# Output projections, dilated-attention values and v: 512-column products over two 512-row weight units in place of 256-column ones

## The chip, the cores and the metric

The kernel runs on one core of a Trainium2 chip. The metric is the device time of one execution in microseconds (us), the median of several runs. The engines are named as in the profile: PE (TensorE, matrix products), PEld (its weight loads), DVE (VectorE), ACT (ScalarE), POOL (GpSimd) and SP (SyncE, which issues the DMAs).

## The reference, cut to what matters

The input x is [1, 1024, 1024] in float32: 1024 tokens of 1024 channels. Three blocks follow each other.

1. `first_block`: a norm, a wide input projection, four mixers side by side (sparse attention, differential attention, retention, a state-space mixer), then `x + mixed @ w_out` and a norm.
2. The second block: an input projection, an RWKV-7 recurrence and a gated convolution side by side, `x + cat @ w_out_2`, and `x + relu(h @ w_ff1)**2 @ w_ff2`, then a norm.
3. The third block works on X = norm(x). A spatial gating branch takes `v = gelu(X @ w_v)` (2048 channels), normalises it, mixes it over tokens and multiplies it with two other projections. A dilated-attention branch has q, k and `vb = X @ w_vb` (1024 channels) for 8 heads. Both go through a projection and a gate each and are summed to m; the output is `x + norm(m @ w_out_3)`.

All matrix products are computed to float32 precision.

## The kernel before

Tokens are cut into 8 tiles of 128 and two halves of 512. An activation that feeds a product stands transposed on chip, as `(hi, lo)`: `hi` is the value rounded to float32r and `lo` the exact rest, each [128, 8 k tiles, 512 tokens] (`act_half`). Weights come in units (`wunit`): one DMA of 1 MB into `wraw`, then ACT makes `whi` (L183) and DVE makes `wlo` (L184), in two halves of 1024 columns each. The unit's three buffers come from a ring of six buffers of 9 KB per partition, so two units fit. A product runs in three passes, hi·hi, hi·lo and lo·hi, for each of its 128-row k tiles (`mm3`, all its matmuls are on L251); with 8 k tiles that is 24 matmuls into one PSUM bank. The profile names a matmul `out<-moving,stationary`.

There are two ways round. `cm` keeps the weights stationary and streams 512 tokens; the result is transposed, and the row reads `mm<-ahi,whi 128x512`. `tm`, and the code in its manner, keeps 128 tokens stationary and streams 256 columns of the weights; the result has tokens on partitions, and the row reads `mm<-whi,ahi 128x256`. Five places use the second way with 256 columns:

- `out_proj` after the first block (called from `first_to_second`): for each of 4 weight units of 256 columns, 4 token tiles, DVE adds the residual (L1629); twice, for two token halves. It is woven step by step with the norms of the next block.
- `out_proj` after RWKV (from `second_to_third`), the same.
- `vb_proj`: pairs of units, for each half and unit 4 token tiles; the result is copied by ACT or DVE (L1722 and L1724) to a buffer `vo` and stored to DRAM (L1725). It is woven with the final norm of block 2, which makes its input X tile by tile.
- `v_proj`: 8 units, for each 8 token tiles; ACT applies GELU (L1924), DVE takes statistics (L1925), SP stores (L1926). It has two PSUM banks.
- the last product of `merge`: ACT squares and sums (L2049), DVE multiplies by the norm's weights (L2050), then come the norm's factor and the output.

PSUM has 8 banks; `set_banks` gives each tag its banks, and `psum(tag)` goes round them. The order of the instructions on each engine is not that of the code: the program is built with a scheduler that plays the program on its own timeline, takes from all code what is ready, and so moves work of one stage into gaps of another. Each engine then executes its list strictly in order, and so does SP's queue of DMA issues. In the RWKV stage, `keep` adds products for nothing that hold their place (L172).

## Time and profile before

| quantity | value |
|---|---|
| runs shown | 3983.67, 3992.8 and 3976.47 us, median 3983.67 |
| profiled execution, span from first to last instruction | 3985.3 us |
| profiled execution, own time outside that span | not listed; the span lies inside the range of the runs |
| PE busy | 3836.2 us, 96% |
| PE weight loads busy | 3287.1 us, 82% |
| DVE, ACT, POOL busy | 2131.0, 1243.3, 539.5 us |
| mean granted TensorE clock | 0.966 of full speed |
| DMA queue 1 | 300.39 MB, 24.3% of 16 engines |

Matmuls overlap in the record: one lasts from its issue to its modelled end, and the next starts before that. So the time that a matmul takes of PE is read from the distance between two starts, not from its duration. The granted clock has two levels, 1.2 GHz (0.5) and 2.4 GHz (1.0).

The five stages of the change lie, in us of the span, at about 748 to 880 (first output projection), 1421 to 1605 (second one, with the end of RWKV), 2292 to 2398 (values of the dilated attention), 2852 to 3064 (v) and 3844 to 3985 (last product). RWKV is at 1131 to 1504.

### The profile page before, as it was taken

What the parts mean: (1) busy time and instruction counts of PE and PEld (TensorE: products, weight loads), DVE (VectorE), ACT (ScalarE), POOL (GpSimd) and SP (SyncE); (2) the same over time, 40 slices, a digit from 0 to 9 for tenths busy, and PEclk for the clock granted to TensorE, in tenths of its full rate; (3) what the DMA queues carried; (4) which work ended last, traced back from release to release, by engine and by line L of the source; (5) the groups of instructions that cost most, each with busy time, mean ns of one, the idle gap of its engine ahead of it and who ended that gap; (6) DMA issues with size and microseconds to landing.
All of it is one profiled execution on the core that took longest, in us unless ns stands there. A gap on an engine that the chain in (4) does not pass through costs nothing.

```text
span 3985.3 us, 57578 instructions
## 1 busy us (share of the span) xinstructions
PE 3836.2 (96%) x22592; PEld 3287.1 (82%) x22592; DVE 2131.0 (53%) x4925; ACT 1243.3 (31%) x2589; POOL 539.5 (14%) x825
## 2 busy tenths in 40 slices
PE   7999999799979989999999999999999999999998
PEld 6788888797868879888888898878899888888897
DVE  5356479668987865544444654444423444433154
ACT  4444436442232434222212232333422111121232
POOL 1011124300043410000000011111201211210000
PEclk9999999799977889999999999999999999999999
DMA  5321342431221233111111132112133222211143
GB/s 147 121 65 51 84 140 73 135 112 55 94 58 38 47 92 120 48 53 43 53 43 53 59 120 59 45 48 59 50 109 92 62 63 60 74 48 48 54 154 121
DMA packets 341697, 304.07 MB, mean 76 GB/s; under 512 B 51182, under 2 KB 305970, under 8 KB 341426
## 3 DMA queue, kind: packets, MB, share of 16 engines
q1 hardware_dynamic: 341426, 300.39, 24.3%
q8 instruction: 178, 2.92, 0.3%
q14 instruction: 93, 0.76, 0.1%
HBM read 234.27 MB, written 61.34 MB: 74 GB/s over the span
## 4 chain that ended last, share of the span: by engine, by line
PE 62%; DVE 2%; DMA 2%; ACT 1%; issue 1%; SPq 0%; POOL 0%; DVEq 0%; ACTq 0%; POOLq 0%
PE mm L251 54%; PE s L1798 2%; PE s L1972 1%; PE o L1820 1%; PE o L1872 1%; PE t L1865 0%; DMA wraw<-in_w_in_dram 0%; PE t L1897 0%; PE t L1842 0%; PE t L213 0%; DVE wlo L184 0%; PE o L1520 0%; PE f L172 0%; DMA alo<-ybT 0%; PE t L1465 0%
## 5 line engine op out<-in xcount | busy, mean ns | idle before, releaser
L251 PE MATMUL mm<-ahi,whi 128*128 128x512 f32 x2464 | 967.1, 394 | 0.5 <-ACT ahi L216 0.5
L251 PE MATMUL mm<-alo,whi 128*128 128x512 f32 x2464 | 965.3, 392 | 0.0
L251 PE MATMUL mm<-ahi,wlo 128*128 128x512 f32 x2464 | 963.4, 391 | 0.3 <-DVE wlo L184 0.3
L251 PE MATMUL mm<-whi,ahi 128*128 128x256 f32 (+2 forms) x1856 | 538.6, 291 | 16.4 <-ACT ahi L1612 7.5
L251 PEld LDWEIGHTS mm<-ahi,whi 128*128 128x128 f32 x2464 | 465.3, 189 | 96.9 <-ACT ahi L216 0.9
L251 PEld LDWEIGHTS mm<-ahi,wlo 128*128 128x128 f32 x2464 | 464.1, 188 | 97.0 <-DVE wlo L184 1.1
L251 PEld LDWEIGHTS mm<-alo,whi 128*128 128x128 f32 x2464 | 464.6, 189 | 94.1 <-issue 0.4
L183 ACT ACTIVATE whi<-wraw 128x1024 fp32r<-128x1024 f32 (+2 forms) x300 | 302.8, 1055 | 765.5 <-DMA wraw<-in_w_ff_dram 318.0
L251 PE MATMUL mm<-wlo,ahi 128*128 128x256 f32 (+2 forms) x1856 | 537.2, 290 | 1.8 <-DVE wlo L184 1.7
L251 PE MATMUL mm<-whi,alo 128*128 128x256 f32 (+2 forms) x1856 | 533.6, 289 | 2.0 <-DVE alo L218 1.5
L184 DVE TENSOR_TENSOR wlo<-wraw,whi 128x1024 fp32r<-128x1024 f32 (+2 forms) x300 | 357.5, 1229 | 332.6 <-PE mm L251 322.4
L251 PEld LDWEIGHTS mm<-whi,ahi 128*128 128x128 f32 x1856 | 358.2, 193 | 24.7 <-ACT ahi L1612 7.9
L251 PEld LDWEIGHTS mm<-wlo,ahi 128*128 128x128 f32 x1856 | 359.2, 194 | 7.6 <-issue 3.8
L251 PEld LDWEIGHTS mm<-whi,alo 128*128 128x128 f32 x1856 | 357.1, 193 | 6.1 <-issue 2.5
L1678 DVE TENSOR_TENSOR xm<-xm,mm 128x512 f32<-128x512 f32 x256 | 173.9, 686 | 120.1 <-PE mm L251 119.9
L251 PE MATMUL mm<-whi,ah 128*128 128x512 f32 x512 | 202.3, 395 | 0.0
L251 PE MATMUL mm<-wlo,ah 128*128 128x512 f32 x512 | 202.1, 395 | 0.0
L251 PE MATMUL mm<-whi,al 128*128 128x512 f32 x512 | 202.1, 395 | 0.0
L1170 DVE SCALAR_TENSOR_TENSOR cva<-cvh,vecs,cva 128x1022 f32<-128x1022 f32 (+29 forms) x120 | 145.4, 1263 | 0.2
L1660 DVE TENSOR_TENSOR fr<-fr 128x512 f32<-128x512 f32 x64 | 44.2, 690 | 154.1 <-ACT fr L1659 154.1
L207 POOL TENSOR_SCALAR x<-x,rT 128x1024 f32<-128x1024 f32 x16 | 18.8, 1174 | 760.9 <-PE mm L251 673.2
L251 PEld LDWEIGHTS mm<-whi,al 128*128 128x128 f32 x512 | 96.5, 188 | 22.5
(577 smaller groups left out, 5786.2 us busy)
## 6 DMA issues: line engine op xcount, KB each, us to landing
wraw<-in_w_in_dram SPq DMA_DIRECT2D x41, 1024.0 KB
wraw<-in_w_ff_dram SPq DMA_DIRECT2D x32, 1024.0 KB
wraw<-in_w_in_dram SPq DMA_DIRECT2D x59, 512.0 KB
wraw<-in_w_out_dram SPq DMA_DIRECT2D x24, 1024.0 KB
gv<-go SPq DMA_DIRECT2D x64, 128.0 KB
vl<-gv SPq DMA_DIRECT2D x16, 512.0 KB
wraw<-in_w_proj_a_dram SPq DMA_DIRECT2D x8, 1024.0 KB
wraw<-in_w_proj_b_dram SPq DMA_DIRECT2D x8, 1024.0 KB
```

The costliest lines, as they stand in the source:

```text
L183: nc.scalar.activation(hi, src, AF.Copy)
L184: nc.vector.tensor_tensor(lo, src, hi.bitcast(F32), op=OP.subtract)
L207: nc.gpsimd.tensor_scalar(xn, xt, rs, 1.0, op0=OP.mult, op1=OP.mult)
L251: nc.tensor.matmul(out, lhs[a][:, kl, ls], rhs[b][:, kr, rs], start=first and n == 0, stop=last and n == tot - 1)
L1170: nc.vector.scalar_tensor_tensor(a[:, 30 - j:], h[:, 0:994 + j], wj, a[:, 30 - j:], op0=OP.mult, op1=OP.add)
L1660: nc.vector.tensor_tensor(r, r, r, op=OP.mult)
L1678: nc.vector.tensor_tensor(xm[t][:, ns], xm[t][:, ns], q, op=OP.add)
L1798: nc.tensor.matmul(q[:, :256], qk[:, a, qcol], qk[:, b, kcol], start=n == 0, stop=n == 2)
L1820: nc.tensor.matmul(ob[:, 128 * (b % 4):128 * (b % 4 + i1 - i0)], vt[:w, cc + 1], pt[:, 128 * i0:128 * i1], start=b % 4 == 0 and cc == b - ...
L1872: nc.tensor.matmul(o[:, 256 * (r % 2):256 * (r % 2) + 256], vg[:, r, kb], pt[:, 256 * kb:256 * kb + 256], start=kb == 0, stop=kb == 1)
L1972: nc.tensor.matmul(q[:, 128 * t:128 * t + 128], vl[:, 4 * hf + t], wt, start=True, stop=True)
```

## The change

In the five places a product streams 512 columns of weights in place of 256. A weight unit still holds 1 MB, but as 512 rows (4 k tiles) by 512 columns in place of 1024 rows by 256 columns. A PSUM tile is now a whole bank and its sum runs over two units: 12 matmuls with the first (`kh == 0`), 12 with the second. `out_proj` and `merge` go over 4 token tiles with one unit, then over the same 4 with the next, so four banks are open at a time. `vb_proj` does so for each half with both units on chip. `v_proj` keeps its two banks and goes over pairs of token tiles. What follows on ACT and DVE is done on 512 columns at a time, except in `vb_proj`, where ACT copies one half of a tile and DVE the other. `merge` gets six banks for its products in place of four. Comments and docstrings are dropped too, which leaves no trace in the program. The diff, cut to its core:

```diff
--- before
+++ after
@@ out_proj, rows of x + A @ w for one token half @@
-    for u in range(4):
-        W = c.wunit([w[:, 256 * u:256 * u + 256]])
-        us = slice(256 * u, 256 * u + 256)
-        for i in range(4):
-            q = c.psum("mm")
-            c.mm3(q[:, :256], A, W, slice(i * 128, i * 128 + 128), slice(0, 256), [(k, k) for k in range(8)])
-            nc.vector.tensor_tensor(xs[i][:, us], xs[i][:, us], q[:, :256], op=OP.add)
-            yield
+    for nh in range(2):
+        ns = slice(512 * nh, 512 * nh + 512)
+        q = []
+        for kh in range(2):
+            W = c.wunit([w[512 * kh:512 * kh + 512, ns]], ktiles=4)
+            for i in range(4):
+                if kh == 0:
+                    q.append(c.psum("mm"))
+                c.mm3(q[i], A, W, slice(i * 128, i * 128 + 128), slice(0, 512), [(4 * kh + k, k) for k in range(4)],
+                      first=kh == 0, last=kh == 1)
+                if kh:
+                    nc.vector.tensor_tensor(xs[i][:, ns], xs[i][:, ns], q[i], op=OP.add)
+                yield
@@ vb_proj @@
-        for g in range(2):
-            W = [c.wunit([self.cols("vb", 256, 256 * u)]) for u in (2 * g, 2 * g + 1)]
+        for nh in range(2):
+            W = [c.wunit([self.cols("vb", 512, 512 * nh)[512 * kh:512 * kh + 512]], ktiles=4) for kh in range(2)]
             for hf in range(2):
-                for i in range(2):
-                    u = 2 * g + i
-                    for t in range(4 * hf, 4 * hf + 4):
-                        q = c.tm(W[i], slice(0, 256), X, t)
-                        o = tmp.tile([128, 256], F32, tag="vo", name=c.nm("vo"), bufs=2)
-                        if t % 2:
-                            nc.vector.tensor_copy(o, q[:, :256])
-                        else:
-                            nc.scalar.activation(o, q[:, :256], AF.Copy)
-                        nc.sync.dma_start(self.vb[t * 128:t * 128 + 128, 256 * u:256 * u + 256], o)
+                q = []
+                for kh in range(2):
+                    for t in range(4):
+                        if kh == 0:
+                            q.append(c.psum("mm"))
+                        c.mm3(q[t], X[hf], W[kh], slice(t * 128, t * 128 + 128), slice(0, 512),
+                              [(4 * kh + k, k) for k in range(4)], first=kh == 0, last=kh == 1)
+                        for i in range(2 * kh):
+                            r = 512 * hf + 128 * t
+                            o = tmp.tile([128, 256], F32, tag="vo", name=c.nm("vo"), bufs=2)
+                            x = q[t][:, 256 * i:256 * i + 256]
+                            if i:
+                                nc.vector.tensor_copy(o, x)
+                            else:
+                                nc.scalar.activation(o, x, AF.Copy)
+                            nc.sync.dma_start(self.vb[r:r + 128, 512 * nh + 256 * i:512 * nh + 256 * i + 256], o)
                         yield
@@ v_proj @@
-        st = p.tile([128, 8, 8, 6], F32, name="vstat")
-        for u in range(8):
-            W = c.wunit([self.cols("v", 256, 256 * u)])
-            for t in range(8):
-                q = c.tm(W, slice(0, 256), X, t)
-                o = p.tile([128, 256], F32, tag="vo", name=c.nm("go"), bufs=3)
-                nc.scalar.activation(o, q[:, :256], AF.Gelu_apprx_tanh)
-                nc.vector.bn_stats(st[:, t, u], o)
-                nc.sync.dma_start(self.gv[t * 128:t * 128 + 128, 256 * u:256 * u + 256], o)
+        st = p.tile([128, 8, 4, 6], F32, name="vstat")
+        for u in range(4):
+            W = [c.wunit([self.cols("v", 512, 512 * u)[512 * kh:512 * kh + 512]], ktiles=4) for kh in range(2)]
+            for t0 in range(0, 8, 2):
+                q = [c.psum("mm") for _ in range(2)]
+                for kh in range(2):
+                    for i in range(2):
+                        t = t0 + i
+                        c.mm3(q[i], X[t // 4], W[kh], slice((t % 4) * 128, (t % 4) * 128 + 128), slice(0, 512),
+                              [(4 * kh + k, k) for k in range(4)], first=kh == 0, last=kh == 1)
+                for i in range(2):
+                    t = t0 + i
+                    o = p.tile([128, 512], F32, tag="vo", name=c.nm("go"), bufs=2)
+                    nc.scalar.activation(o, q[i], AF.Gelu_apprx_tanh)
+                    nc.vector.bn_stats(st[:, t, u], o)
+                    nc.sync.dma_start(self.gv[t * 128:t * 128 + 128, 512 * u:512 * u + 512], o)
@@ merge, its last product; third_block @@
-            for u in range(4):
-                us = slice(256 * u, 256 * u + 256)
-                W = c.wunit([ins["w_out_3"][0][:, us]])
-                for i in range(4):
-                    q = c.psum("mm")
-                    c.mm3(q[:, :256], mh, W, slice(i * 128, i * 128 + 128), slice(0, 256), [(k, k) for k in range(8)])
-                    sq = tmp.tile([128, 256], BF, tag="fsq", name=c.nm("sq"), bufs=1)
...
+            for nh in range(2):
+                ns = slice(512 * nh, 512 * nh + 512)
+                q = []
+                for kh in range(2):
+                    W = c.wunit([ins["w_out_3"][0][512 * kh:512 * kh + 512, ns]], ktiles=4)
+                    for i in range(4):
+                        if kh == 0:
+                            q.append(c.psum("mm"))
+                        c.mm3(q[i], mh, W, slice(i * 128, i * 128 + 128), slice(0, 512), [(4 * kh + k, k) for k in range(4)],
+                              first=kh == 0, last=kh == 1)
...
+        c.set_banks(mm=[0, 1, 2, 3, 6, 7], t=[4, 5])
         with pool("mrg") as tmp:
             b.merge(ps, out, tmp)
```

How the order moves, at three places. First PE at the start of the first output projection, where products of `out_proj` (mm, weights whi and wlo, activations ahi and alo) are put between the last steps of differential attention (o, t), and of the state-space mixer (do; its result is turned by L824). Before:

```order
L251 MATMUL mm_8430<-wlo_8343,ahi_8313 128x256
L251 MATMUL mm_8430<-whi_8342,alo_8314 128x256
L788 MATMUL o_7021<-vv_5997,dAT_7221 128x64
L770 MATMUL t_7252<-ident,ws_6027 128x128 x4
L1051 MATMUL do_8247<-ws_5998,xbcB_7753 128x64 x4
L1054 MATMUL do_8247<-sst_8230,xbcB_7753 128x128 x2
L770 MATMUL t_7259<-ident,ws_6027 128x128
L788 MATMUL o_7021<-vv_5997,dAT_7257 128x64 x4
L251 MATMUL mm_8464<-whi_8457,ahi_8313 128x256
L788 MATMUL o_7021<-vv_5997,dAT_7261 128x64
```

Now:

```order
L251 MATMUL mm_8391<-wlo_8343,ahi_8313 128x512
L251 MATMUL mm_8391<-whi_8342,alo_8314 128x512
L788 MATMUL o_7021<-vv_5997,dAT_7221 128x64
L770 MATMUL t_7252<-ident,ws_6027 128x128 x4
L1051 MATMUL do_8247<-ws_5998,xbcB_7753 128x64 x4
L1054 MATMUL do_8247<-sst_8230,xbcB_7753 128x128 x2
L770 MATMUL t_7259<-ident,ws_6027 128x128
L788 MATMUL o_7021<-vv_5997,dAT_7257 128x64 x4
L788 MATMUL o_7021<-vv_5997,dAT_7261 128x64
L251 MATMUL mm_8475<-whi_8468,ahi_8313 128x512
```

The 20 products that stand between the two L788 rows (the last two of them are shown) have kept their places at twice the width. Before the turn L824, six products of the next column unit have become one.

The second place is ACT in `v_proj`: GELU results `go`, and the splits of weight units. Before:

```order
L1924 ACTIVATE go_26557<-mm_26532 128x256
L1868 ACTIVATE mpg_26316<-t_26311 128x512
L1924 ACTIVATE go_26586<-mm_26561 128x256
L1924 ACTIVATE go_26623<-mm_26598 128x256
L183 ACTIVATE whi_27071<-wraw_27070 128x1024 x2
L1924 ACTIVATE go_26652<-mm_26627 128x256
L1924 ACTIVATE go_26681<-mm_26656 128x256
L1924 ACTIVATE go_26710<-mm_26685 128x256
L1924 ACTIVATE go_26739<-mm_26714 128x256
```

Now:

```order
L1942 ACTIVATE go_25300<-mm_25250 128x512
L1879 ACTIVATE mpg_25084<-t_25079 128x512
L1942 ACTIVATE go_25304<-mm_25251 128x512
L1942 ACTIVATE go_25358<-mm_25308 128x512
L183 ACTIVATE whi_25375<-wraw_25374 128x1024 x2
L1942 ACTIVATE go_25362<-mm_25309 128x512
L1974 ACTIVATE wt_26163<-t_26161 128x128
L183 ACTIVATE whi_25615<-wraw_25614 128x1024 x2
L1942 ACTIVATE go_25432<-mm_25382 128x512
```

Before, one unit's split stands within a run of eight GELUs, a whole unit ahead of its use. Now a unit's split stands at the end of its pair's predecessor: whi_25375 is the second half of the rows for the next 512 columns, whose first product is go_25432's.

The third place is POOL in the RWKV stage, whose code is unchanged: lnx and lny belong to the convolution's norm, all others to RWKV. Before:

```order
L1233 TENSOR_SCALAR lnx_11646<-lnx_11646 128x512
L1234 TENSOR_TENSOR lny_11649<-lny_11649,lnx_11646 128x512
L1340 TENSOR_SCALAR ws_11287<-ws_11287 128x512
L1373 TENSOR_TENSOR ws_11287<-ws_11287 128x512
L1346 TENSOR_SCALAR ws_11289<-ws_11287,vecs_625,ka_11271 128x128 x4
L1233 TENSOR_SCALAR lnx_11683<-lnx_11683 128x512
L1234 TENSOR_TENSOR lny_11686<-lny_11686,lnx_11683 128x512
L1377 TENSOR_TENSOR ws_11285<-rk_11882,rk_11883 128x512
L1423 COPY ws_11288<-ws_11286 64x256
```

Now:

```order
L1361 TENSOR_TENSOR ws_10871<-ws_10871,s_2316_11549 128x512
L1234 TENSOR_TENSOR lny_11233<-lny_11233,lnx_11230 128x512
L1340 TENSOR_SCALAR ws_10871<-ws_10871 128x512
L1373 TENSOR_TENSOR ws_10871<-ws_10871 128x512
L1346 TENSOR_SCALAR ws_10873<-ws_10871,vecs_625,ka_10855 128x128 x4
L1377 TENSOR_TENSOR ws_10869<-rk_11466,rk_11467 128x512
L1233 TENSOR_SCALAR lnx_11267<-lnx_11267 128x512
L1423 COPY ws_10872<-ws_10870 64x256
L1385 TENSOR_TENSOR ws_10873<-ws_10873,ws_10871 128x512
```

The work is the same, but from here on the scheduler has put the RWKV steps of POOL, ACT, DVE, PE and SP in another sequence.

## Rows read from the trace of the kernel before

**Rows 1.** The page of the whole run: busy time by engine, and 40 slices.
```profile
PE 3836.2 (96%) x22592; PEld 3287.1 (82%) x22592; DVE 2131.0 (53%) x4925; ACT 1243.3 (31%) x2589; POOL 539.5 (14%) x825
...
PEclk9999999799977889999999999999999999999999
```

**Rows 2.** Groups by line and form, engine PE: count, busy us, mean ns.
```profile
L251 PE MATMUL mm<-whi,ahi 128*128 128x256 f32 x1536 | 440.2, 288 | 12.0 <-ACT ahi L1612 7.5 <-ACT whi L183 2.1 <-DVE y L1577 0.8
L251 PE MATMUL mm<-wlo,ahi 128*128 128x256 f32 x1536 | 438.4, 286 | 1.8 <-DVE wlo L184 1.7
L251 PE MATMUL mm<-whi,alo 128*128 128x256 f32 x1536 | 435.8, 286 | 2.0 <-DVE alo L218 1.5 <-DVE alo L1613 0.5
```

**Rows 3.** Timeline of PE in the v stage (start us, duration us, instruction).
```profile
2899.80 0.28 PE L251 MATMUL mm<-wlo,ahi 128*128 128x256 f32 x1
...
2906.52 0.28 PE L251 MATMUL mm<-whi,ahi 128*128 128x256 f32 x1
```

**Rows 4.** Timeline of PE in the last stage, 512 columns.
```profile
3799.74 0.39 PE L251 MATMUL mm<-ahi,wlo 128*128 128x512 f32 x1
...
3805.86 0.39 PE L251 MATMUL mm<-alo,whi 128*128 128x512 f32 x1
```

**Rows 5.** Timeline of PE in the feed-forward's second product.
```profile
1999.61 0.40 PE L251 MATMUL mm<-whi,al 128*128 128x512 f32 x1
...
2002.41 0.40 PE L251 MATMUL mm<-whi,al 128*128 128x512 f32 x1
```

**Rows 6.** Timeline of PE at the first output projection's start.
```profile
755.06 0.41 PE L251 MATMUL mm<-whi,ahi 128*128 128x256 f32 x1
...
758.69 0.41 PE L251 MATMUL mm<-whi,alo 128*128 128x256 f32 x1
```

**Rows 7.** Waits there: engine and line that waited <- releaser: us, times, longest.
```profile
PE mm L251 <- ACT ahi L1612: 6.8, 1, 6.8
...
PE ds L824 <- DVE ssm_y L1096: 6.6, 1, 6.6
```

**Rows 8.** Stretches: width, busy us (count) of PE, PEld, DVE, ACT, POOL, clock.
```profile
1131.00:1465.00 334.00, 296.30 (x3293) 253.48 (x3293) 267.30 (x660) 125.94 (x283) 124.56 (x164) 0.80 0.22 53
...
2292.00:2348.00 56.00, 53.19 (x434) 51.57 (x433) 42.72 (x158) 27.78 (x77) 10.77 (x12) 1.00 0.27 96
...
2896.00:3066.00 170.00, 169.62 (x1378) 167.46 (x1377) 48.34 (x97) 34.85 (x72) 0.00 (x0) 1.00 0.34 107
...
3840.00:3985.40 145.40, 131.89 (x927) 123.97 (x925) 70.89 (x113) 43.66 (x97) 0.00 (x0) 0.96 0.38 128
```

**Rows 9.** Waits in the stretch 2292 to 2348 us.
```profile
POOL x L207 <- DVE rR L168: 31.1, 3, 17.7
```

**Rows 10.** Weight loads in the v stage: duration ns min/median/max, first and last start.
```profile
L184 DVE TENSOR_TENSOR wlo<-wraw,whi x16: 1218/1222/1226, 2893.5 to 3061.7; 128x1024 fp32r<-128x1024 f32 x16
L183 ACT ACTIVATE whi<-wraw x14: 1042/1050/1059, 2900.1 to 3042.8; 128x1024 fp32r<-128x1024 f32 x14
L233 SPq DMA_DIRECT2D wraw<-in_w_in_dram x9: 383/384/427, 2894.5 to 3036.5; - x9
```

**Rows 11.** Groups by line: the 512-column GELU from PSUM.
```profile
L1965 ACT ACTIVATE ug<-mm 128x512 f32<-128x512 f32 x32 | 18.8, 589 | 18.9 <-PE mm L251 18.9
```

**Rows 12.** The page, group of the feed-forward's 512-column add from PSUM.
```profile
L1678 DVE TENSOR_TENSOR xm<-xm,mm 128x512 f32<-128x512 f32 x256 | 173.9, 686 | 120.1 <-PE mm L251 119.9
```

**Rows 13.** Timeline of the end: last square and last product with g_post.
```profile
3972.28 0.38 ACT L2049 ACTIVATE sq<-mm 128x256 bf16<-128x256 f32 x1 [2.40 <-PE mm L251]
...
3972.78 0.42 DVE L2050 TENSOR_TENSOR pa<-mm,gpost 128x256 f32<-128x256 f32 x1 [2.45 <-ACT sq L2049]
```

**Rows 14.** Waits in the RWKV stage.
```profile
POOL ws L1340 <- ACT ws L1339: 41.7, 10, 12.8
```

More of the change, by code (lines that the diff above doesn't have):

```diff
@@ L2036, in merge @@
             v2 = lambda a: a.rearrange("p (a b) -> p a b", a=2)
-            ms = tmp.tile([128, 4, 4], F32, tag="fms", name=c.nm("fms"), bufs=2)
+            ms = tmp.tile([128, 4, 2], F32, tag="fms", name=c.nm("fms"), bufs=2)
             xs = [self.gb[:, 2 * i:2 * i + 2, hs] for i in range(4)]
@@ L2041, in merge @@
                 nc.sync.dma_start(xs[i], v2(self.x3[t * 128:t * 128 + 128]))
-            for u in range(4):
-                us = slice(256 * u, 256 * u + 256)
-                W = c.wunit([ins["w_out_3"][0][:, us]])
-                for i in range(4):
-                    q = c.psum("mm")
-                    c.mm3(q[:, :256], mh, W, slice(i * 128, i * 128 + 128), slice(0, 256), [(k, k) for k in range(8)])
-                    sq = tmp.tile([128, 256], BF, tag="fsq", name=c.nm("sq"), bufs=1)
-                    nc.scalar.activation(sq, q[:, :256], AF.Square, accum_out=ms[:, i, u:u + 1])
-                    nc.vector.tensor_tensor(ys[i][:, u // 2, 256 * (u % 2):256 * (u % 2) + 256], q[:, :256], gp[:, us],
-                                            op=OP.mult)
+            for nh in range(2):
[8 more added lines that the diff above has]
+                              first=kh == 0, last=kh == 1)
+                        if kh == 0:
+                            continue
+                        sq = tmp.tile([128, 512], BF, tag="fsq", name=c.nm("sq"), bufs=1)
+                        nc.scalar.activation(sq, q[i], AF.Square, accum_out=ms[:, i, nh:nh + 1])
+                        nc.vector.tensor_tensor(ys[i][:, nh], q[i], gp[:, ns], op=OP.mult)
             m = c.sm([128, 4])
```

## The prediction, made before the changed kernel ran

> **What bounds the kernel now.** I read the page first. PE is busy 96% of the span and its clock is at the 2.4 GHz level in nearly every slice but those around RWKV [rows 1], so what PE executes sets the time wherever it does not wait. The table of stretches says where that holds: in the v stage PE is busy 169.62 of 170 us at full clock, while between 2292 and 2348 us 2.8 us are idle, and RWKV's 334 us have 37.7 us idle at a mean clock of 0.80 [rows 8]. Then the groups by form: 3 x 1536 = 4608 matmuls stream 256 columns [rows 2]. They are all that the change touches, and 2304 matmuls of 512 columns replace them. The mean of 286 to 288 ns is not their price, since they overlap. The price is the distance between two starts, which I take from the timeline.
>
> **The price of a column.** With 256 columns there are 56 steps from 2899.80 to 2906.52 us: 6.72/56 = 120.0 ns [rows 3]. Streaming 256 columns at 2.4 GHz is 106.7 ns, so each matmul carries 13.3 ns that do not depend on its columns. With 512 columns, 27 steps from 3799.74 to 3805.86 us give 226.7 ns, which is 213.3 + 13.3 [rows 4]. So two narrow matmuls take 240.0 ns and a wide one 226.7 ns: 13.3 ns saved per pair, at most 2304 x 13.3 = 30.7 us. But the trace has a second price for 512 columns. In the feed-forward's second product, 12 steps from 1999.61 to 2002.41 us give 233.3 ns [rows 5]. There the weights move and the activations stand still, as in the changed code, and a sum has only 6 matmuls; in rows 4 the weights stand still and a sum has 24. The change has 12 per visit of a bank and 24 per sum. These two rows are my bounds; both lie under 240, so I exclude a loss at full clock. I take 226.7: weights moved by 256 columns cost the same 13.3 ns on top, so that their moving alone is not what is dear, and the number per sum is that of rows 4.
>
> At the 1.2 GHz level nothing is saved: 17 steps from 755.06 to 758.69 us give 213.5 ns, which is 256 columns at 1.2 GHz with nothing on top [rows 6].
>
> The Trainium skill, TensorE: Matmul & The Clock Gate, section "Back-to-back issue gap", puts a warm gap at N/2.4 plus about 2.5 ns, so that halving the number of matmuls would save only 2.5 ns each, 5.8 us in all. The trace does not agree: it shows 13.3 ns on top at both widths [rows 3, 4].
>
> **Stage by stage** (times are savings).
>
> First output projection. The order shows 36 narrow matmuls issued before the third pair of k tiles arrives, and 26 wide ones now. 732 x 120.0 = 87.8 us remain of 768 narrow ones, 358 x 226.7 = 81.2 us of 384 wide ones: 6.7 us. Against it, 20 of the early ones stand in PE's list ahead of the last steps of differential attention and of the state-space mixer, now twice as wide. The end of that chain is waited for twice: 6.6 us for ssm_y, then 6.8 us for the activations loaded after it [rows 7]. Both waits move by as much as PE is late: 20 x 106.7 = 2.1 us if the added columns run at 2.4 GHz, 20 x 213.5 = 4.3 us at 1.2 GHz. I take 3.2, the middle, since the clock there changes within the block. Saved: 3.5 us.
>
> Second output projection. 148 narrow matmuls are placed within the end of RWKV before, 75 wide ones now, the same columns; they fill RWKV's gaps and give nothing. The other 620 x 120.0 = 74.4 us become 309 x 226.7 = 70.1 us. Saved: 4.3 us.
>
> Values of dilated attention (vb). 384 pairs would give 5.1 us. Half of them run while the final norms make X tile by tile, and that chain sets the pace: POOL waits there 31.1 us for the norms' factors alone, and PE has 2.8 us idle [rows 8, 9]. What PE saves there it waits. Saved: 2.6 us.
>
> v. 768 pairs x 13.3 = 10.2 us, in a stretch where PE has no gap [rows 8]. What could open one is the weights. Before, a unit's DMA was issued at 2894.5 us and its split began at 2900.1, 5.6 us later; half a split takes 1.05 us on ACT and 1.22 on DVE [rows 10]. Now the second unit of each pair is loaded when the first unit of the pair before is done, and needed after 12 + 12 + 12 + 12 = 48 matmuls, 10.9 us. It is ready after 5.6 + 1.05 + 1.22 = 7.9 us, so 3 us of cover remain. If it were gone, each of three handovers would cost what is missing. The GELU of 512 columns takes 0.59 us [rows 11] against 2.7 us before its bank is wanted. It may stand behind a split of 2.1 us in ACT's list, so I give up 0.5 us. Saved: 9.7 us.
>
> Last product. 384 pairs: 5.1 us. The end of the kernel hangs on the last tile: its square takes 0.38 us and its product with the norm's weights 0.42 [rows 13]; for 512 columns, 0.59 on ACT and 0.69 on DVE [rows 11, 12], so 0.5 us more on the path. The six banks change nothing where PE has no gap. Saved: 4.6 us.
>
> Residual adds, statistics and stores are done in half as many, larger pieces on engines that wait for PE; they cost nothing while PE is the bound. vb's stores are as many as before.
>
> RWKV. Its code is the same, its order is not (third place in the section on the change). No row shows what another order costs. A single wait there is at most 12.8 us long [rows 14]; one such wait won or lost are my bounds, and I take 0, since I see no reason for a sign.
>
> Sum: 3.5 + 4.3 + 2.6 + 9.7 + 4.6 = 24.7 us. It is made against the profiled execution's span of 3985.3 us. What lies around that span isn't listed, and is small, since the median of the runs is 3983.67, 1.6 us below. Taken off the median: **3959 us**.
>
> **Rivals.**
>
> 1. The wide matmul costs 233.3 ns, as in rows 5. Then 6.7 ns per pair are saved. First projection: 87.8 - 358 x 0.2333 = 4.3, less 3.2, is 1.1; second: 74.4 - 72.1 = 2.3; vb 1.3; v 5.1 - 0.5 = 4.6; last 2.6 - 0.5 = 2.1. Sum 11.4 us: 3972 us. For it speaks that the roles of the operands are those of rows 5; against it, that 256 moved weight columns cost no more on top than rows 4 show.
>
> 2. RWKV's new order lowers its clock, and the kernel is slower. The stage's mean clock is 0.80 where PE has 37.7 us idle, against 1.00 in v, where it has none [rows 8], and the keep products were put where the old order had gaps. If PE's 296.3 busy us scale with the clock, the gain of 24.7 is gone at 0.80 x 296.3/321.0 = 0.738. At 0.70 the stage is 42 us longer: 4001 us. Against it: the keep products hold their places among their own steps, and the stage has many waits on ACT and POOL that do not scale.
>
> 3. What is on top belongs to the columns, so that a wide matmul with moved weights costs 240.0 ns, as two narrow ones. Then nothing is saved, and the delays of 3.2, 0.5 and 0.5 us stay: 3988 us. Against it, a wide matmul shows 226.7 and 233.3 ns [rows 4, 5], never 240. The skill's gap rule quoted above ends near this rival, with 5.8 us saved.
>
> **How the numbers follow.** About 0.5% (19.9 us) is what a measurement of this kernel can tell from no change. The forecast has 0.60: with RWKV between -12.8 and +12.8 it runs from 3946 to 3972, and 0.52 of it lies below 3963.8. Rival 1 has 0.20, 3959 to 3985 with the same bounds: 0.03 faster, 0.17 the same. Rival 2 has 0.07: 0.06 slower, 0.01 the same. Rival 3 has 0.02, the same. The remaining 0.11 is a larger shift by the new order, either way: 0.05 faster, 0.05 the same, 0.01 slower. Sums: faster 0.60, same 0.33, slower 0.07. The likeliest case's own range is 3946 to 3972. The range for all reaches into rival 1 above, and below by a few us for a larger gain in RWKV: 3942 to 3981.
>
> **What would show it.** 2304 fewer matmuls, and starts of `mm<-whi,ahi 128x512` 226.7 ns apart in the v stage: then the v stage is 10 us shorter and the last one 5. If they are 233 ns apart, rival 1 holds. The wait for ssm_y ends 2 to 4 us later than before, counted from the block of 20. In vb the idle time of PE grows. RWKV, from 1131 us to the last of its products, keeps its length within 12.8 us and its clock within 0.80 ± 0.03; outside that, the order decides and the sum above is only a part. Gaps of PE at the start of a v column block would show the weights late.

## The result, and the profile after

| | median of the runs | runs | lowest to highest |
|---|---|---|---|
| kernel before, on the same chip | 3986.76 us | 10 | 3976.47 to 3998.59 |
| changed kernel | 3961.64 us | 10 | 3955.85 to 3977.27 |

The ratio is 0.9945, 95% interval 0.9935 to 0.9956: faster by 22 us, 18 to 26; the two medians lie 25.1 us apart. The profiled execution has a span of 3956.6 us against 3985.3, which is 28.7 us less. That is one run beside one run; how much of it is chance is worked out below.

The page after, busy time by engine and the granted clock in 40 slices, as [rows 1]:

```profile
PE 3795.8 (96%) x20288; PEld 3149.7 (80%) x20288; DVE 2112.9 (53%) x4845; ACT 1231.0 (31%) x2521; POOL 540.1 (14%) x825
...
PEclk9999998899978999999999999999999999999999
```

PE has 2304 instructions less, as many as the change replaces. It is still busy 96% of the span, so it is still the bound. The groups that take the place of [rows 2]:

```profile
L251 PE MATMUL mm<-whi,ahi 128*128 128x512 f32 x768 | 301.8, 397 | 17.0 <-ACT whi L183 8.2 <-ACT ahi L1612 7.9 <-DVE y L1577 0.8
L251 PE MATMUL mm<-wlo,ahi 128*128 128x512 f32 x768 | 301.6, 393 | 0.1
L251 PE MATMUL mm<-whi,alo 128*128 128x512 f32 x768 | 301.2, 394 | 1.6 <-DVE alo L218 1.6
```

The forms with 256 columns are gone from these three groups. What a matmul of 512 columns costs now is read from the starts, here PE in the v stage (start us, duration us, instruction):

```profile
2929.67 0.39 PE L251 MATMUL mm<-whi,ahi 128*128 128x512 f32 x1
...
2937.38 0.39 PE L251 MATMUL mm<-wlo,ahi 128*128 128x512 f32 x1
```

34 steps in 7.71 us are 226.8 ns, against 120.0 for 256 columns [rows 3] and the 226.7 of [rows 4]. Two stretches of the changed kernel, the v stage and the last stage from the first to the last wide matmul (columns as [rows 8]):

```profile
2892.00:3035.00 143.00, 142.93 (x634) 117.90 (x633) 39.25 (x52) 26.88 (x40) 0.00 (x0) 1.00 0.33 108
...
3812.19:3942.91 130.72, 130.72 (x577) 107.96 (x575) 65.04 (x84) 39.26 (x63) 0.00 (x0) 1.00 0.40 133
```

PE has no gap in either, at full clock. From 2840 to 2892 us, where v begins, PE is busy 52.00 of 52 us as well. So the weights of v's column blocks are not late. Their handling there (duration ns min/median/max, first and last start), beside [rows 10]:

```profile
L184 DVE TENSOR_TENSOR wlo<-wraw,whi x15: 1218/1224/1227, 2896.9 to 3039.1; 128x1024 fp32r<-128x1024 f32 x15
...
L183 ACT ACTIVATE whi<-wraw x14: 1042/1053/1061, 2902.8 to 3039.0; 128x1024 fp32r<-128x1024 f32 x14
```

A split takes what it took before: 1.22 us on DVE, 1.05 on ACT.

At the first output projection PE waits twice, as before [rows 7], but the first wait has another name (start, duration, instruction, idle before and releaser):

```profile
767.98 0.79 PE L251 MATMUL mm<-whi,ahi 128*128 128x512 f32 x1 [7.10 <-ACT whi L183]
768.65 1.09 PE L824 MATMUL ds<-ident,ssm_y 128*128 128x128 f32 x4
...
779.39 0.80 PE L251 MATMUL mm<-whi,ahi 128*128 128x512 f32 x1 [7.93 <-ACT ahi L1612]
```

PE now stops one instruction earlier, at a product whose weights ACT splits only after its part of the state-space mixer's norm. The turn L824 then begins 19.0 us after the projection's first product (749.62 us), in the profile before 19.5 us after it (751.25).

After vb comes a wait that is 0.32 us long in the profile before and 1.85 us now:

```profile
2374.79 0.39 PE L251 MATMUL mm<-alo,whi 128*128 128x512 f32 x1
2377.03 0.57 PE L251 MATMUL mm<-ahi,wlo 128*128 128x512 f32 x1 [1.85 <-DVE wlo L184]
2377.39 0.63 PE L251 MATMUL mm<-ahi,whi 128*128 128x512 f32 x1
2377.82 0.63 PE L251 MATMUL mm<-alo,whi 128*128 128x512 f32 x1
```

PE stands still until DVE has made `wlo` of the next unit. Then eight matmuls stand 0.43 us apart, at the clock's lower level, until 2380.8 us. The wait is 1.0 to 2.3 us in all nine profiles with a wide vb (in e1_vb and e3_out1 in two parts, the first of them for DVE's copy of a tile of vb); the slow matmuls stand in only three of them (`after`, e1_vb and e3_u256), not in e2_split, whose wait is the longest. From vb's last product to the first scores of the modulated attention it took 22.2 us before and 25.3 now.

The norm chain beside vb, from 2280 to 2330 us (waits: us in total, times, longest), answers to [rows 9]:

```profile
POOL x L207 <- DVE rR L168: 25.2, 2, 17.6
```

The norms' factors are still what POOL waits for longest, here in 50 us, there 31.1 us in 56.

The end, as [rows 13] (the last square now takes 0.60 us, the last product with the norm's weights 0.69):

```profile
3943.01 0.60 ACT L2073 ACTIVATE sq<-mm 128x512 bf16<-128x512 f32 x1 [2.03 <-PE mm L251]
...
3943.73 0.69 DVE L2074 TENSOR_TENSOR pa<-mm,gpost 128x512 f32<-128x512 f32 x1 [2.03 <-ACT sq L2073]
```

### Stage by stage, over all profiles

One profile beside one profile does not do here: the stretch up to the first output projection has the same instructions on PE in all 13 profiles, and takes from 745.1 to 755.2 us. So I cut each trace at the same instructions and compare stages over all of them. The columns, in us: out1, from the first to the last product of the first output projection; rwkv, from there to RWKV's last product (L1576); out2, from there to the last product of the second output projection; vb, from its first product to the first scores of the modulated attention; mod+v+gate, from there to the last product of y_a; last, first to last product of `merge`'s last; tail, from there to the end.

```
             out1    rwkv   out2      vb  mod+v+gate    last   tail
before     123.97  622.18  82.64  124.59     1202.24  136.40  13.07
e1_last    120.20  621.39  82.43  124.62     1202.19  130.72  13.55
e1_v       120.83  618.93  82.61  124.61     1192.52  136.59  13.21
e1_vb      121.53  620.25  82.63  122.47     1201.43  136.84  13.07
e1_out     118.46  623.18  76.43  125.29     1205.23  135.95  13.22
after      116.88  623.49  77.79  120.43     1195.08  130.72  13.68
e2_split   116.64  622.45  76.62  119.15     1196.30       -      -
e2_visit6  116.61  624.80  77.12  119.15     1192.63  130.72  13.71
e2_sum6    116.45  622.88  76.37  118.75     1196.07  130.72  14.46
e2_banks4  117.80  622.89  77.88  118.11     1194.45  130.72  13.69
e3_out1    116.75  627.44  82.63  122.68     1194.83  130.72  13.68
e3_u256    116.65  623.09  77.97  120.07     1196.47  130.72  14.45
e4_out2    123.95  614.74  77.90  118.39     1194.93  130.72  13.53
```

The feed-forward between out2 and vb takes 711.3 to 711.4 us in all of them. Means over the profiles that are wide and narrow in a stage (all five places wide where a stage depends on others: `after`, the four e2 runs and e3_u256; e1_out is left out of the narrow means of vb and mod+v+gate, and with it they give -5.5 and -7.6) give: out1 122.1 to 117.0, -5.1; rwkv 620.7 to 623.3, +2.6; out2 82.6 to 77.3, -5.3; vb 124.6 to 119.3, -5.3; mod+v+gate 1202.0 to 1195.2, -6.8; last 136.4 to 130.7, -5.7; tail +0.6. The sum is -25.0 us, which is the difference of the two medians (25.1) and lies within the interval.

How much is chance shows in profiles that share one order of instructions. The first projection takes 120.2 to 124.0 us in the five where it is narrow, RWKV 618.9 to 622.2 in the four with both projections narrow, and mod+v+gate 1192.6 to 1196.5 in the seven that have the changed kernel's order there. So one profile against one, in these three stages, tells nothing below about 4 us. The e2 and e3 kernels ran once each; only their stages are read, not their whole time.

### The profile page after: what moved, and what is told of

Same layout as the page of the kernel before. It is cut to its first block, busy times and chain, and to the rows that moved or that the text cites. A ratio compares the mean times of both kernels' runs of the same rounds, so it can differ in the third digit from the quotient of the medians.

```text
span 3956.6 us, 52689 instructions
## 1 busy us (share of the span) xinstructions
PE 3795.8 (96%) x20288; PEld 3149.7 (80%) x20288; DVE 2112.9 (53%) x4845; ACT 1231.0 (31%) x2521; POOL 540.1 (14%) x825
## 4 chain that ended last, share of the span: by engine, by line
PE 87%; DVE 6%; DMA 3%; ACT 1%; issue 1%; SPq 1%; POOL 1%; DVEq 0%; ACTq 0%; POOLq 0%
PE mm L251 71%; PE s L1809 2%; DMA wraw<-in_w_in_dram 1%; PE s L532 1%; PE t L568 1%; PE o L1831 1%; PE s L1990 1%; PE o L1883 1%; DVE ws L738 1%; PE t L213 1%; PE o L578 1%; PE o L579 1%; SPq L1439 1%; PE s L1403 0%; PE s L531 0%
## 5 line engine op out<-in xcount | busy, mean ns | idle before, releaser
L251 PEld LDWEIGHTS mm<-ahi,whi 128*128 128x128 f32 x2464 | 465.8, 189 | 96.3 <-issue 0.4
L251 PE MATMUL mm<-whi,ahi 128*128 128x512 f32 (+2 forms) x1088 | 400.2, 371 | 21.1 <-ACT whi L183 8.2
L251 PE MATMUL mm<-whi,alo 128*128 128x512 f32 (+2 forms) x1088 | 399.0, 368 | 1.6 <-DVE alo L218 1.6
L251 PE MATMUL mm<-wlo,ahi 128*128 128x512 f32 (+2 forms) x1088 | 400.4, 368 | 0.1
L251 PEld LDWEIGHTS mm<-whi,ahi 128*128 128x128 f32 x1088 | 206.6, 190 | 57.1 <-ACT whi L183 8.7
L251 PEld LDWEIGHTS mm<-wlo,ahi 128*128 128x128 f32 x1088 | 206.5, 190 | 35.2 <-issue 3.8
L251 PEld LDWEIGHTS mm<-whi,alo 128*128 128x128 f32 x1088 | 206.0, 189 | 35.2 <-issue 2.5
L1815 POOL TENSOR_SCALAR mS<-mS,s 128x256 f32<-128x256 f32 x128 | 60.8, 478 | 405.2 <-DVE s L1814 337.8
```

The lines of the kernel that those rows point to most:

```text
L251: nc.tensor.matmul(out, lhs[a][:, kl, ls], rhs[b][:, kr, rs], start=first and n == 0, stop=last and n == tot - 1)
L1815: nc.gpsimd.tensor_scalar(S_, S_, r, 1.0, op0=OP.mult, op1=OP.mult)
```

## The experiments

The theory: 13.3 ns go with each matmul that goes, wherever PE does not wait, and the rest of the kernel is only shifted (theory A). The rivals: the gain is the order and clock of RWKV, or the banks, or waits take its place. First each part of the change alone.

**e1_last**: the kernel before, with `merge` and its six banks from the change.

```diff
-            for u in range(4):
+            for nh in range(2):
+                    W = c.wunit([ins["w_out_3"][0][512 * kh:512 * kh + 512, ns]], ktiles=4)
+        c.set_banks(mm=[0, 1, 2, 3, 6, 7], t=[4, 5])
```

> The kernel before with only the last product of merge (and its six banks) wide. Theory A (each of the 384 matmuls that go away takes 13.3 ns with it, wherever PE does not wait): the order ahead of this stage is as before, so first to last matmul of the last stage falls from 136.4 us to 131 to 131.5, the tail grows by 0.5 to 0.6 us, the whole by -4.5 us, ratio 0.9988 or 0.9989. Rival B (the gain of the full change is order and clock in RWKV, which only happens to be there): the stage is shorter as the trace of the full change shows, but the whole is within 2 us. Rival C (the two extra banks, not the width, made the last stage shorter): cannot be told apart by this run alone.

Measured: 0.9989 (0.9980 to 0.9997), tail +0.5. From the first to the last product, in the kernel before and here (columns as [rows 8]):

```profile
3835.78:3972.18 136.40, 136.11 (x961) 128.19 (x959) 67.34 (x100) 43.59 (x95) 0.00 (x0) 1.00 0.39 128
```

```profile
3830.63:3961.35 130.72, 130.72 (x577) 107.92 (x575) 65.11 (x84) 39.32 (x63) 0.00 (x0) 1.00 0.39 133
```

130.72 us for 577 matmuls, all of 512 columns, are 226.6 ns each. That is theory A's size: 384 x 13.3 = 5.1 us, and the 0.3 us of idle time that the profile before has there are gone too; 0.3 of the 5.7 us are left over. The whole, 1 to 8 us shorter, is too wide an interval to decide against rival B's 2 us; the stage decides the price.

**e1_v**: the kernel before, with `v_proj` from the change.

```diff
-        for u in range(8):
-            W = c.wunit([self.cols("v", 256, 256 * u)])
+        for u in range(4):
+            W = [c.wunit([self.cols("v", 512, 512 * u)[512 * kh:512 * kh + 512]], ktiles=4) for kh in range(2)]
```

> The kernel before with only v_proj wide. Theory A: 768 matmuls less; from the first scores of the modulated attention to the last matmul of v (644.7 us before, 635.3 with the full change) 9.2 to 10.2 us less; whole about 10 us shorter, ratio 0.9975. Rival B: whole within 3 us, because the weights of a column block come late (gaps at the start of each block) or the modulated attention gives the time back.

Measured: 0.9980 (0.9970 to 0.9990). To v's last product 632.8 us in place of 644.7; but ten matmuls of the next stage have moved behind v's last, 2.2 us, so with the gate stage it is 1192.5 against 1202.0 (the narrow mean), -9.4. That is within theory A's 9.2 to 10.2. The whole is 8 us shorter, 4 to 12, more than the 3 of rival B.

**e1_vb**: the kernel before, with `vb_proj` from the change.

```diff
-            W = [c.wunit([self.cols("vb", 256, 256 * u)]) for u in (2 * g, 2 * g + 1)]
+            W = [c.wunit([self.cols("vb", 512, 512 * nh)[512 * kh:512 * kh + 512]], ktiles=4) for kh in range(2)]
```

> The kernel before with only vb_proj wide. Theory A: first to last matmul of vb from 102.4 us to about 97 to 95; the full change showed 95.1 and then a wait of 1.9 us and 3.4 us at the half clock where the next product begins. If that wait belongs to vb's wide units, it is here too and the whole gains 3 to 5 us, ratio 0.9990; if it belongs to another part of the change, the whole gains 5 to 7 us, ratio 0.9985.

Measured: 0.9997 (0.9985 to 1.0009), not to be told from no change. vb itself is 5.4 us shorter, the way from there to the modulated attention 3.3 us longer: 2.1 us remain. PE waits there 1.35 and 0.40 us, so the handover's wait belongs to vb's wide units. With the second projection wide as well, vb to the modulated attention gains 5.3 us: the parts do not add up. Part of it is the clock. With a wide vb behind a narrow second projection (e1_vb and e3_out1), vb has a mean granted clock of 0.98 and 0.97, and PE is busy 95.1 and 96.3 us from its first to its last product; in the seven profiles where the second projection is wide too, 1.00 and 93.3 to 93.5 us.

**e1_out**: the kernel before, with `out_proj` from the change, in both its calls.

```diff
-    for u in range(4):
-        W = c.wunit([w[:, 256 * u:256 * u + 256]])
+    for nh in range(2):
+            W = c.wunit([w[512 * kh:512 * kh + 512, ns]], ktiles=4)
```

> The kernel before with only out_proj wide, both calls. Theory A: first call's span 124.0 to 117 us, last matmul of the second 4 to 5 us after RWKV's end earlier, and RWKV's length 622.2 within 2 us: whole 11 to 13 us shorter, ratio 0.9970. Rival B (order): RWKV's new order alone is worth more than 5 us in either direction, and the whole is off by as much from 12 us. The sum of the four parts should come to 24 to 28 us by theory A.

Measured: 0.9994 (0.9984 to 1.0004). Expected by theory A was 0.9970: here the theory of a mere shift falls. The two projections are shorter, by 3.6 and 6.2 us against the narrow means, but RWKV is 2.5 us longer and the stages from the modulated attention to the gate, whose code is that of the kernel before, 3.3 us (one profile). Both stretches have another order of instructions than in the kernel before; in RWKV the four profiles with narrow projections share one order line for line, but for two neighbouring matmuls in one of them. The four ratios multiply to 0.9960, the whole change has 0.9945; their intervals overlap.

Next the price itself, in the last stage, where nothing comes behind that could be reordered.

**e2_split**: the changed kernel; 192 of the wide matmuls in two parts.

```diff
-                        c.mm3(q[i], mh, W, slice(i * 128, i * 128 + 128), slice(0, 512), ...
+                        for cs in ((slice(0, 384), slice(384, 512)) if kh else (slice(0, 512),)):
+                            c.mm3(q[i][:, cs], mh, W, slice(i * 128, i * 128 + 128), cs, ...
```

> The changed kernel; in the last product, the second half of each sum (192 of the 384 wide matmuls) is done as 192 of 384 columns and 192 of 128. Theory A (13.3 ns on top of the columns, whatever the width): steps of 173.3 and 66.7 ns, 240.0 ns for the two, the last stage 2.6 us longer than 130.7. Rival (a matmul has a floor, since each brings its own weights: the 128x64 products o<-vv,dAT of differential attention stand 112 ns apart): 128 columns take about 110 ns, and the stage is 10 to 11 us longer. Rival (the price on top belongs to the columns): 170 and 57 ns, no change.

```profile
3848.36 0.33 PE L251 MATMUL mm<-wlo,ahi 128*128 128x384 f32 x1
...
3849.58 0.33 PE L251 MATMUL mm<-whi,alo 128*128 128x384 f32 x1
...
3849.81 0.27 PE L251 MATMUL mm<-wlo,ahi 128*128 128x128 f32 x1
...
3850.93 0.28 PE L251 MATMUL mm<-whi,alo 128*128 128x128 f32 x1
```

Seven steps of 384 columns in 1.22 us: 174 ns, as a price of 13.3 on top says. Ten steps of 128 columns in 1.12 us: 112 ns, not 66.7. From the last product's start to the kernel's end it takes 155.9 us, 11.5 more than in `after` (144.4), a little over the 10 to 11 of the rival with a floor. That rival was right: 13.3 ns on top hold from 256 columns up (the products of 288 columns elsewhere in the kernel before stand 133 ns apart: 120.0 + 13.3), and for 128 there is a floor near 111. It is the floor of a stream: in each row of twelve the first 128-column step takes 60 ns, the others 110 to 114, and the weight loads start about 111 ns apart there. Between 128 and 256 columns no width was tried.

The Trainium skill, TensorE: Matmul & The Clock Gate, section "LDWEIGHTS (loading the stationary operand)", has a weight load take its columns over 1.2 in ns, an estimate of 107 ns for 128. The trace is near it: each matmul here loads its own weights (20288 loads for 20288 matmuls), and the floor is 111. The Trainium skill's section "Back-to-back issue gap" of TensorE: Matmul & The Clock Gate gives 81 ns at 128 columns and 131 at 512 for a sustained stream, and the N/2.4 + 2.5 that the prediction quotes for an isolated matmul; the runs, with 112 and 226.7 ns, agree with neither.

**e2_visit6** and **e2_sum6**: the changed kernel; the last product goes round its banks every 6 matmuls, and in e2_sum6 each 6 are a sum of their own that DVE adds to the row.

```diff
+                for kk in range(4):
+                        c.mm3(q[i], mh, W[kk // 2], ..., [(2 * kk + k, 2 * (kk % 2) + k) for k in range(2)], first=kk == 0, last=kk == 3)
```

```diff
+                        q = c.psum("mm")
+                        c.mm3(q, mh, W[kk // 2], ..., [(2 * kk + k, 2 * (kk % 2) + k) for k in range(2)], first=True, last=True)
+                            nc.vector.tensor_tensor(ys[i][:, nh], ys[i][:, nh], q, op=OP.add)
```

> The changed kernel; the last product goes round its four banks in visits of 6 matmuls in place of 12, sums of 24 as before. If going to another bank is what makes the feed-forward's second product take 233 ns per matmul, the steps are 230 to 233 ns here and the last stage 1.3 to 2.6 us longer than 130.7. If it is not, 226.7 ns and no change.

> The changed kernel; the last product in sums of 6 matmuls, each of which DVE copies or adds to the row at once, as in the feed-forward's second product. If the short sum, or DVE reading and writing beside it, is what makes that product take 233 ns per matmul, the steps are 231 to 235 ns and the last stage is 2 to 3 us longer than 130.7 (the chain behind the last sum longer too, by about 1.5 us). If the feed-forward's price comes from elsewhere (its own splits and loads), 226.7 ns.

Measured: 226.7 ns and 130.72 us in both; the tail of e2_sum6 is 0.8 us longer than that of `after`, about half of what was expected. Neither the visit nor the short sum makes the second price of [rows 5].

**e3_u256**: the changed kernel; the last product with the feed-forward's units and sums.

```diff
+            for kk in range(4):
+                W = c.wunit([ins["w_out_3"][0][256 * kk:256 * kk + 256, :]], ktiles=2)
```

> The changed kernel; the last product is done with the feed-forward's units, 256 rows by 1024 columns, in sums of 6 that DVE adds to the row. If that shape of unit (2 k tiles of 1024 columns) is what makes the feed-forward's second product and y_a @ w_proj_a take 233 ns per matmul, the steps are 231 to 235 ns and the last stage 2 to 3 us longer than 130.7. If it is not, they stay at 226.7 ns, as in the run with sums of 6, and the cause lies in what else those stages do at the time.

```profile
3825.72 0.39 PE L251 MATMUL mm<-whi,alo 128*128 128x512 f32 x1
...
3832.29 0.39 PE L251 MATMUL mm<-wlo,ahi 128*128 128x512 f32 x1
```

29 steps in 6.57 us are 226.6 ns, and the stage takes 130.72 us. The unit's shape is not it either.

**e2_banks4**: the changed kernel without the six banks.

```diff
-        c.set_banks(mm=[0, 1, 2, 3, 6, 7], t=[4, 5])
```

> The changed kernel without the six banks for merge (mm on 0 to 3, as before). With PE never waiting for a bank, the last stage stays at 130.7 us within 0.3. If the banks are what lets it run without gaps, PE waits for the squares and products of the first column half at the start of the second: up to 4 gaps of 0.5 to 1.3 us per half, 2 to 8 us in all.

Measured: 130.72 us. The banks do nothing here, so what e1_last gained is not theirs.

Last, where the order's cost comes from: the two calls of `out_proj` one by one.

**e3_out1**: the changed kernel, its second output projection narrow. **e4_out2**: the first one narrow. `out_proj_n` is `out_proj` as in the kernel before.

```diff
-                rows = lambda hf: out_proj(c, A[hf], c.ins["w_out_2"][0], x2, ...
+                rows = lambda hf: out_proj_n(c, A[hf], c.ins["w_out_2"][0], x2, ...
```

```diff
-        rows = lambda hf: out_proj(c, A[hf], c.ins["w_out"][0], c.ins["x"][0], ...
+        rows = lambda hf: out_proj_n(c, A[hf], c.ins["w_out"][0], c.ins["x"][0], ...
```

> The changed kernel with the second output projection narrow again (256 columns, two units of 1024 rows), the first one wide. In six profiles with both wide, RWKV's stretch from the last product of the first projection took 622.4 to 624.8 us, in four with both narrow 618.9 to 622.2. If the second projection's wide products, placed in RWKV's end, are what makes its new order dearer, the stretch comes back to 619 to 622 here and the second projection's end behind RWKV takes 82 to 83 us in place of 76 to 78. If it is the first projection's new timing that shifts RWKV's order, the stretch stays at 622.5 to 625. The same for the modulated attention, whose stretch to v's last product is 3 us longer with both wide.

> The changed kernel with the first output projection narrow again, the second one wide: the fourth of the four combinations. RWKV's stretch took 620.7 us (mean) with both narrow, 623.3 with both wide, 627.4 with only the first wide. Theory (the first call's timing sets RWKV's order, the second's wide products in RWKV's end are worth about 4 us there): 616 to 618 us here, the first projection back at 120 to 122 us, and the whole within 4 us of the changed kernel, ratio to before 0.993 to 0.9955. Rival (the two interact by chance of the order): RWKV 620 us or more, and the whole 2 to 6 us slower than the changed kernel, ratio 0.995 to 0.997.

The stretch from the first projection's last product to RWKV's, in the kernel before, in the changed kernel, in e3_out1 and in e4_out2 (width, then busy us and count of PE, PEld, DVE, ACT, POOL, clock):

```profile
875.21:1497.40 622.19, 569.37 (x4597) 479.78 (x4595) 502.21 (x1016) 198.45 (x410) 145.02 (x186) 0.88 0.23 65
```

```profile
866.50:1490.00 623.50, 563.12 (x4524) 466.92 (x4522) 496.59 (x1018) 199.43 (x412) 145.34 (x186) 0.90 0.23 65
```

```profile
866.64:1494.08 627.44, 566.47 (x4596) 473.59 (x4595) 496.68 (x1021) 199.54 (x412) 145.70 (x186) 0.89 0.22 64
```

```profile
878.20:1492.94 614.74, 560.37 (x4524) 467.25 (x4522) 502.44 (x1013) 198.64 (x410) 145.61 (x186) 0.90 0.23 66
```

With both narrow the mean is 620.7 us. Only the first wide costs 6.7 us there, only the second wide gains 6.0, both together cost 2.6. The two runs of one narrow call are one profile each, and both missed their expectation: 622.5 to 625 was expected for e3_out1, 616 to 618 for e4_out2. Whose order it is, is plain: in e3_out1 POOL runs the stretch in the changed kernel's order, line for line, and in e4_out2 in that of the kernel before; ACT, DVE and PE differ from these at a few places. So the first call's timing sets RWKV's order, as the theory had it. The second call's wide products give 4 us back (627.4 to 623.3) or 6 (620.7 to 614.7). The longest waits in 334 us from 1122.3 and from 1134.0 us, in the changed kernel and in e4_out2:

```profile
ACT X L1481 <- PE t L1480: 52.4, 11, 9.3
POOL ws L1340 <- ACT ws L1339: 46.8, 8, 15.3
...
POOL Sc L1518 <- DVE Tc L1534: 26.3, 6, 9.7
```

```profile
POOL ws L1340 <- ACT ws L1339: 41.0, 10, 12.1
POOL Sc L1518 <- DVE Tc L1534: 40.0, 8, 8.6
ACT X L1481 <- PE t L1480: 36.7, 8, 11.2
```

In the dearer order ACT waits 15.7 us longer for PE's turns and POOL 5.8 us longer for ACT, but POOL 13.7 us less for DVE. What remains on PE is read from the stretches above: 52.8 us without work in the kernel before, 60.4 in the changed kernel, 61.0 in e3_out1, 54.4 in e4_out2. Which single step of the order costs it was not tried. e4_out2 as a whole has 0.9941 (0.9927 to 0.9954), the changed kernel 0.9945 (0.9935 to 0.9956): what it loses in the first projection (7.1 us in its profile, whose 124.0 is above the 120 to 122 expected) it has back in RWKV. It is no better version that could be told from the changed kernel.

## Why the prediction was right, point by point

Predicted 24.7 us, measured 22 (18 to 26). The main term, the price of a column, holds to the nanosecond; of the stages, three gained some 1 to 3 us more than forecast, and RWKV and the modulated attention gave about as much back. So the price is understood, while the closeness of the sum is in part luck: the errors of the stages come to +5.8 and -5.5 us.

**The price.** 226.7 ns in all five stages, wherever wide matmuls follow each other at full clock. Rival 1 (233.3) and rival 3 (240) are refuted by e1_last alone. [Rows 5] were a true price of another stage, not a bound on this one. What makes it remains open, below.

**First projection**, predicted 3.5, measured 5.1. The 6.7 of saved steps are there; of the delay of 3.2 us there is little. The step failed in that I let both waits move by what PE is late. Over the profiles, the turn L824's last instruction comes 18.1 to 21.0 us after the projection's first product when narrow (mean 19.61) and 20.5 to 22.2 when wide (20.95): 1.3 us later, where 2 to 4 were forecast.

**RWKV**, predicted 0 within 12.8, measured +2.6. Its clock rose from 0.80 to 0.83 in the stretch of [rows 8] moved to the same place (1120 to 1460 us), so rival 2 failed in its sign; but PE's idle time rose with it and took more than the clock gave: from the first projection's end to RWKV's last product PE is busy 563.1 us in place of 569.4, and idle 60.4 in place of 52.8.

**Second projection**, predicted 4.3, measured 5.3.

**vb**, predicted 2.6, measured 5.3 with the handover. I took the norm chain as setting the pace and PE as waiting for what it saves. But the chain is no fixed pace: its turns (L213) stand in PE's own list, between vb's matmuls. From vb's first product to the last norm it took 51.8 us before and 48.9 now, and PE's idle time in vb fell from 2.8 to 1.6 us where I expected it to grow. That the quicker PE is what made the chain shorter is not shown: with vb wide and the second projection narrow it took 50.7 us (e1_vb) and 52.8 (e3_out1). The wait behind vb was missing from the sum.

**v**, predicted 9.7; alone it gives 9.4. In the whole change 6.8 remain, and the loss is not v's. From v's first product to the end of the gate stage the means are 765.3 us narrow and 755.6 wide: 9.7, as forecast. The loss lies ahead of v, in the modulated attention. From its first scores to v's first product it takes 436.2 to 436.9 us in the four profiles with both projections narrow and 437.5 to 440.4 in the nine others, 3.0 us more in the mean. I had counted such a cost for RWKV only. That another order causes it is not shown: seven of the nine share one order on PE, DVE, ACT and POOL and fill that whole range, and e1_vb, with an order of its own, takes 436.9. The weights were in time, as the sum of 7.9 us against 10.9 said.

**Last product**, predicted 4.6, measured 5.1 (5.7 less a tail of 0.6).

## What to carry to other kernels

Where PE has no gap, count its instructions and take the step between starts at both widths from the trace; the fixed part times the instructions removed is the gain of that stage (10.2 us by the count and 9.7 measured in v, 5.1 and 5.7 in the last product). For the whole kernel the sum of 24.7 us came out within 3 of the 22 measured, with errors of the stages that happened to cancel. Where a scheduler orders the work, a stage whose code is untouched can win or lose as much as the edit itself (RWKV: -6.0 to +6.7 us for an edit worth 6.7 in the first projection, in single profiles), so try the parts in all combinations before you call one of them good. Where the part of the kernel ahead of the edit varies by more than the effect, cut the traces at the same instructions and compare stages.

## What the runs showed of the hardware

In a stream of matmuls that each bring their own 128 columns of weights, there is a floor near 111 ns between starts: 128 moving columns cost almost what 256 do (112 ns in e2_split, 120.0 in the kernel before).

The feed-forward's second product still stands apart. In the changed kernel 28 steps there, from the first line to the last (PE, start us), take 232 ns each:

```profile
2012.25 0.40 PE L251 MATMUL mm<-whi,ah 128*128 128x512 f32 x1
...
2018.75 0.40 PE L251 MATMUL mm<-wlo,ah 128*128 128x512 f32 x1
```

They repeat with a period of seven matmuls (241, 232, 231, 232, 228, 230, 233 ns), alike in all 13 profiles for most of the feed-forward, although a sum has six. Sums of six, visits of six and units of 256 rows do not bring it about elsewhere (e2_sum6, e2_visit6, e3_u256: 226.7 ns). The y_a product of the gate shows 233 to 234 ns too. What the two share, activations in a tile of two k tiles by 1024 tokens, was not tried; in e3_u256 only the weights lay so. The cause stays open. One period of seven gives 232.4 ns, so it is worth an estimated 1536 x 5.7 ns = 9 us in the feed-forward.
